# The inputs of a convolution transposed by VectorE and a DRAM round trip instead of TensorE, in a two-layer decoder trunk on one core

## The chip, the core and the metric

The kernel runs on one NeuronCore of a Trainium2 chip. Its engines each work through their own list of instructions in order: TensorE (PE; PEld is its weight load), VectorE (DVE), ScalarE (ACT), GpSimd (POOL) and SyncE (SP), which here issues nearly all DMAs. The metric is the device time of one execution in microseconds.

## The reference

A trunk of two layers over 256 tokens of width 1024, in float32. Each layer is a feed-forward block, a mixer and a second feed-forward block. The mixer projects the tokens once and splits the columns; one branch is a Mamba-2 scan, whose inputs go through a causal convolution of 4 taps over the tokens, one filter per channel (1536 channels):

```python
q, k, v, z, xbc, dt_raw, u, vg, gate_raw = jnp.split(xn @ w_in, split_at, axis=-1)
y_a = moba_attention(q, k, v)
xbc = jax.nn.silu(causal_depthwise_conv(xbc, conv_w, conv_b))
xs, bm, cm = jnp.split(xbc, [SSM_WIDTH, SSM_WIDTH + SSM_GROUPS * SSM_STATE], axis=-1)
y_s = ssd_scan(xs, dt, a, bm, cm) + d_skip[:, None] * xs
y_s = rms_norm(y_s.reshape(b_, s, SSM_WIDTH) * jax.nn.silu(z), ssm_norm_g)
```

## The kernel before

The 256 tokens are two tiles (`t` = 0, 1) of 128. Every product of activations and weights is made of three matmuls of 128x512 (`unit`, L213 to L215), because both operands are split into a high and a low part: `hi*hi + lo*hi + hi*lo`. The weights come in blocks of 128x1024 (512 KB). For each block SP loads `raw` (L160), ScalarE makes `whi` from it (L180) and VectorE `wlo` (L181). There are 6 `raw` buffers and 11 pairs of parts; the split of a new block waits for TensorE to be through with the block whose pair it takes, and the load of a new `raw` waits for the `wlo` that frees its buffer. A block is 12 matmuls on TensorE.

Everything else runs as tasks beside these matmuls. The order on every engine is the order in which the code is run through: after each unit (6 matmuls, counted as 1.3 us) `pump` lets the tasks go on whose waits have run out, then starts at most one split. The wait after a `yield` comes from the table `W` (`x0` 0.65, `cv` 5.2, `cs` 6.5, `out` 6.5, `in` 6.5, and so on). `finish` runs a task to its end at once, whatever its waits: what is left of it is then written in one piece into the engines' lists.

In the mixer, `project` makes 512 columns at a time into PSUM. First come two chunks of `xbc` together, then `conv(0)` and `conv(1)` are spawned; then the third chunk, and `conv(2)`; then two chunks of `z` (4 blocks each); then `finish(*cv)` (L910), and on to `q`. One `conv`:

1. `tokens` (L504, ScalarE) scales the two PSUM tiles into `xtok`, 128 tokens x 512 channels each.
2. `transposed` (L513 TensorE, L516 ScalarE) turns them by four 128x128 transposes a tile into the PSUM tile `ctr` and copies that into `xc`, channels x tokens.
3. ScalarE scales `xc` by the last tap (L535, four instructions), VectorE adds the three shifted taps (L541, six instructions, a wait, six more), ScalarE applies the SiLU (L544).
4. For chunks 0 and 1, eight transposes on TensorE (L552, `xstr`) and two copies on ScalarE (L553) bring the result back to tokens x channels; for chunk 2, two transposes (L559, `btr`) and a copy (L561).

The feed-forward blocks have a transpose of another kind: `swap_out` and `swap_in` (L277 to L286). VectorE transposes 32x32 blocks inside a 128x512 tile, SP writes the tile to DRAM and reads it back with the blocks in their places.

Of the kernel before, what the change touches and what calls it, by code (L numbers as in the profile page):

```python
# [9 lines left out]
F32 = mybir.dt.float32  # L10
# [6 lines left out]
P = 128  # L17
L = 2
S = 256
NT = S // P  # L20
# [27 lines left out]
W = {'gw': 6.5, 'tr': 0, 'parts': 0, 'sq': 1.3, 'lead': 3.9, 'sq2': 5.2, 'hh': 5.2, 'x0': 0.65, 'cv': 5.2, 'cs': 6.5, 'xs': 0, 'dt1': 2.6, 'dt2': 0, 'dt3': 5.2, 'cb': 2.6, 'w1': 1.3, 'w2': 5.2, 'ys': 3.9, 'qk': 3.9, 'vv': 0, 'qs': 0, 'ex': 0, 'p1': 10.4, 'p2': 0, 'p3': 3.9, 'ge': 0, 'ln': 10.4, 'sv': 0, 'yc': 9.1, 'mg': 3.9, 'out': 6.5, 'in': 6.5}  # L48
# [3 lines left out]
def trunk(ctx, tc, a):  # L52
    nc = tc.nc
    V, A, G, T = nc.vector, nc.scalar, nc.gpsimd, nc.tensor
# [5 lines left out]
    dram = ctx.enter_context(tc.tile_pool(name="dram", bufs=1, space=bass.MemoryType.DRAM))  # L60
# [3 lines left out]
    def b4(name, shape=(P, 1024), dt=F32):  # L64
        return big.tile(list(shape), dt, name=name, tag="b4", bufs=B4)

    def b2(name, shape=(P, 512), dt=F32):
        return big.tile(list(shape), dt, name=name, tag="b2", bufs=B2)
# [15 lines left out]
    def tr(name):  # L84
        return psum.tile([P, 512], F32, name=name, tag="tr", bufs=TR)
# [196 lines left out]
    def swap_in(dst, rd):  # L282

        v = rd.rearrange("(a i) (c e) -> c i a e", a=4, c=4)
        for c in range(4):
            nc.sync.dma_start(dst[32 * c:32 * c + 32], v[c])  # L286

    def halves(ps, hi, lo):

        p3 = ps.rearrange("p (k t) -> p k t", k=4)  # L290
        A.copy(hi, p3)
        V.tensor_tensor(lo, p3, hi.bitcast(F32), op=ALU.subtract)
# [185 lines left out]
    def mixer(l, x, r2, nxt):  # L478
# [20 lines left out]
        def tokens(ps, scales, name):  # L499

            out = []
            for t in range(NT):
                o = b2(name)
                A.activation(o, ps[t], AF.Copy, scale=scales[t])  # L504
                out.append(o)
            return out

        def transposed(toks, place, eng):

            for t in range(NT):  # L510
                ps = tr("ctr")
                for j in range(4):
                    T.transpose(ps[:, j * P:(j + 1) * P], toks[t][:, j * P:(j + 1) * P], ident)  # L513
                p3 = ps.rearrange("p (k t) -> p k t", k=4)
                if eng == "a":
                    A.copy(place(t), p3)  # L516
                else:
                    V.tensor_copy(place(t), p3)
                yield W["tr"]
# [6 lines left out]
        def conv(c, ps):  # L526
            toks = tokens(ps, r2, "xtok")
            xc = b4("xc", (P, 4, S))
            yield W["x0"]
            yield from transposed(toks, lambda t: xc[:, :, t * P:(t + 1) * P], "a")  # L530
            o = b4("conv", (P, 4, S))
            w = lambda j, k: pl[:, G_CW + 4 * (4 * c + j) + k:G_CW + 4 * (4 * c + j) + k + 1]
            for j in range(4):
                ct = 4 * c + j
                A.activation(o[:, j, :], xc[:, j, :], AF.Identity, scale=w(j, 3),  # L535
                             bias=pl[:, G_CB + ct:G_CB + ct + 1])
            for jj in (0, 2):
                for k in range(3):
                    s = 3 - k
                    for j in (jj, jj + 1):  # L540
                        V.scalar_tensor_tensor(o[:, j, s:], xc[:, j, :S - s], w(j, k), o[:, j, s:],  # L541
                                               op0=ALU.mult, op1=ALU.add)
                yield W["cv"]
            A.activation(o, o, AF.Silu)  # L544
            yield W["cs"]
            if c < 2:
                for t in range(NT):
                    if t not in xs:
                        xs[t] = b4(f"xs{t}")
                    pt = tr("xstr")  # L550
                    for j in range(4):
                        T.transpose(pt[:, j * P:(j + 1) * P], o[:, j, t * P:(t + 1) * P], ident)  # L552
                    A.copy(xs[t][:, 512 * c:512 * c + 512], pt)  # L553
                    yield W["xs"]
            else:
                bc["T"] = o
                pt = tr("btr")
                for g in range(SG):
                    T.transpose(pt[:, g * P:(g + 1) * P], o[:, g, 0:P], ident)  # L559
                bc["b"] = b2("btok", (P, SG * P))  # L560
                A.copy(bc["b"], pt[:, :SG * P])  # L561
# [184 lines left out]
        def attention(yax, free):  # L746
            for t in range(NT):
# [33 lines left out]
                for g in range(2):  # L781
                    yield W["p1"]
                    pts = {}
                    for k in range(t + 1):
                        pt = tr("ptr")
                        for j in range(4):
                            T.transpose(pt[:, j * P:(j + 1) * P], sc[g][:, j, k * P:(k + 1) * P], ident)
                        pts[k] = b2("pT", (P, 4, P))
                        A.copy(pts[k], pt.rearrange("p (h q) -> p h q", h=4))
                        yield W["p2"]  # L790
                    yield W["p3"]
                    po = tr("pv")
                    for j in range(4):
                        hh = 4 * g + j
                        for k in range(t + 1):
                            T.matmul(po[:, j * P:(j + 1) * P], vv[k][:, hh * HD:(hh + 1) * HD], pts[k][:, j, :],
                                     start=k == 0, stop=k == t)
                    halves(po, hi[:, 4 * g:4 * g + 4, :], lo[:, 4 * g:4 * g + 4, :])
# [106 lines left out]
        for c, ps in enumerate(project("xbc", head=HOLD, nch=2)):  # L905
            cv.append(spawn(conv(c, ps)))
        factors()
        cv.append(spawn(conv(2, project("xbc")[0])))
        ze = [spawn(z_evac(c, project("z")[0])) for c in range(2)]
        finish(*cv)  # L910
# [224 lines left out]
```

## Time and profile before

| | |
|---|---|
| median of three runs | 1486.49 us (1485.8 to 1487.09) |
| the profiled execution | 1487.98 us, of which the span of instructions is 1486.2 us |
| TensorE busy | 1472.1 us, 99% of the span |
| VectorE, ScalarE busy | 955.2 us (64%), 782.6 us (53%) |
| DMA | 293.37 MB, a mean of 197 GB/s |

The page gives for each engine the time in which it was busy, and the chain of work that ended last, followed back from the end: which engine each piece of it was spent on. Times inside the profile count from the first instruction. The convolutions of the first layer lie between 215 and 253 us, those of the second between 950 and 988 us.

### The profile page before, as it was taken

The page shows a single profiled execution, that of the slowest core. Times are in us where ns is not written, and L with a number is a line of the kernel's source. Part 1 is how long each engine was busy: PE and PEld are TensorE (multiplying, and loading weights), DVE is VectorE, ACT ScalarE, POOL GpSimd, SP SyncE. Part 2 cuts the span into 40 slices and gives each one's busy share as a digit, 9 for nine tenths or more (in the row PEclk, how much of TensorE's full clock was granted, in tenths as well). Part 3 has the DMA queues.
Part 4 walks back from the last instruction along what each step waited for, and adds up shares of the span by engine and source line. Part 5 has one row for each costly group of instructions (what it writes and reads, how often), then busy time and mean ns, then how long its engine had stood idle before and what let it go on. Part 6 is the DMA issues. An engine that isn't in the chain of part 4 may idle for free.

```text
span 1486.2 us, 18786 instructions
## 1 busy us (share of the span) xinstructions
PE 1472.1 (99%) x6850; PEld 1218.8 (82%) x6850; DVE 955.2 (64%) x1160; ACT 782.6 (53%) x1079; POOL 55.6 (4%) x98
## 2 busy tenths in 40 slices
PE   9999999999999999999999999999999999999998
PEld 7888888878888888888888888888788888888886
DVE  6766477766666857656486564876665667676652
ACT  6644367555374536544364543765554645464441
POOL 0000020000000000000000000200000000000000
PEclk9999999999999999999999999999999999999999
DMA  8987655335556445888568784654354564478860
GB/s 291 323 253 236 199 190 179 127 115 184 159 181 217 168 154 198 283 230 259 163 230 256 235 253 132 224 167 135 119 192 141 194 204 170 134 272 261 238 200 29
DMA packets 112476, 293.37 MB, mean 197 GB/s; under 512 B 16896, under 2 KB 41600, under 8 KB 112384
## 3 DMA queue, kind: packets, MB, share of 16 engines
q1 hardware_dynamic: 111808, 291.84, 60.6%
q8 instruction: 54, 0.88, 0.2%
q10 hardware_dynamic: 576, 0.33, 0.1%
q14 instruction: 38, 0.31, 0.1%
HBM read 279.54 MB, written 12.58 MB: 197 GB/s over the span
## 4 chain that ended last, share of the span: by engine, by line
PE 94%; DVE 4%; ACT 1%; issue 1%; POOL 0%; DMA 0%; DVEq 0%; ACTq 0%; POOLq 0%
PE gu L213 11%; PE gu L215 11%; PE gu L214 11%; PE dn L213 5%; PE dn L215 5%; PE dn L214 5%; PE br L213 3%; PE br L215 3%; PE br L214 3%; PE gate L215 2%; PE gate L213 2%; PE gate L214 2%; DVE wlo L181 2%; PE xbc L215 1%; PE xbc L213 1%; PE xbc L214 1%
## 5 line engine op out<-in xcount | busy, mean ns | idle before, releaser
L181 DVE TENSOR_TENSOR wlo<-raw,whi 128x1024 fp32r<-128x1024 f32 x495 | 600.2, 1232 | 331.1 <-ACT whi L180 319.8
L180 ACT CAST whi<-raw 128x1024 fp32r<-128x1024 f32 x495 | 512.8, 1051 | 380.9 <-PE gu L215 131.8
L213 PE MATMUL gu<-whi,xh 128*128 128x512 f32 x704 | 276.0, 392 | 1.4 <-ACT xh L316 1.4
L214 PE MATMUL gu<-wlo,xh 128*128 128x512 f32 x704 | 274.9, 391 | 0.0
L215 PE MATMUL gu<-whi,xl 128*128 128x512 f32 x704 | 274.8, 390 | 0.0
L213 PEld LDWEIGHTS gu<-whi,xh 128*128 128x128 f32 x704 | 132.7, 188 | 29.8 <-ACT xh L316 1.8
L215 PEld LDWEIGHTS gu<-whi,xl 128*128 128x128 f32 x704 | 132.6, 188 | 28.0 <-DVE xl L317 0.4
L214 PEld LDWEIGHTS gu<-wlo,xh 128*128 128x128 f32 x704 | 132.5, 188 | 27.9 <-DVE wlo L169 0.9
L213 PE MATMUL dn<-whi,hTh 128*128 128x512 f32 x352 | 137.5, 391 | 0.0
L215 PE MATMUL dn<-whi,hTl 128*128 128x512 f32 x352 | 137.0, 389 | 0.0
L214 PE MATMUL dn<-wlo,hTh 128*128 128x512 f32 x352 | 136.9, 389 | 0.0
L215 PEld LDWEIGHTS dn<-whi,hTl 128*128 128x128 f32 x352 | 66.1, 188 | 13.8
L213 PE MATMUL gate<-whi,xh 128*128 128x512 f32 x192 | 77.3, 403 | 0.0
L214 PEld LDWEIGHTS dn<-wlo,hTh 128*128 128x128 f32 x352 | 66.1, 188 | 13.5
L213 PEld LDWEIGHTS dn<-whi,hTh 128*128 128x128 f32 x352 | 66.1, 188 | 13.4
L215 PE MATMUL gate<-whi,xl 128*128 128x512 f32 x192 | 75.0, 391 | 0.0
L214 PE MATMUL gate<-wlo,xh 128*128 128x512 f32 x192 | 74.8, 390 | 0.0
L316 ACT CAST xh<-xg 128x512 fp32r<-128x512 f32 (+1 forms) x25 | 15.1, 603 | 62.3 <-DVE xg L314 62.3
L215 PEld LDWEIGHTS gate<-whi,xl 128*128 128x128 f32 x192 | 36.0, 188 | 7.7
L405 ACT ACTIVATE silu<-gu,r 128x512 f32<-128x512 f32 (+1 forms) x48 | 31.3, 654 | 19.8 <-PE gu L215 16.2
L214 PEld LDWEIGHTS gate<-wlo,xh 128*128 128x128 f32 x192 | 36.2, 188 | 6.6
L213 PEld LDWEIGHTS gate<-whi,xh 128*128 128x128 f32 x192 | 36.1, 188 | 6.6
(243 smaller groups left out, 2248.3 us busy)
## 6 DMA issues: line engine op xcount, KB each, us to landing
raw<-in_mix SPq DMA_DIRECT2D x232, 512.0 KB, 4.2
raw<-in_gu SPq DMA_DIRECT2D x175, 512.0 KB, 4.9
raw<-in_dn SPq DMA_DIRECT2D x88, 512.0 KB, 4.5
swap<-xt SPq DMA_DIRECT2D x40, 256.0 KB, 3.2
hr<-swap SPq DMA_DIRECT2D x160, 64.0 KB, 4.9
row_ffn_post_g<-in_ffn_post_g SPq DMA_DIRECT2D x4, 512.0 KB, 7.0
swap<-xt SPq DMA_DIRECT2D x8, 128.0 KB, 4.4
hr<-swap SPq DMA_DIRECT2D x32, 32.0 KB, 6.1
```

The costliest lines, as they stand in the source:

```text
L180: A.copy(hi, w)
L181: V.tensor_tensor(lo, w, hi.bitcast(F32), op=ALU.subtract)
L213: T.matmul(o, xh(k, t), hi[:, off:off + n], start=first, stop=False)
L214: T.matmul(o, xh(k, t), lo[:, off:off + n], start=False, stop=False)
L215: T.matmul(o, xl(k, t), hi[:, off:off + n], start=False, stop=last)
L316: A.copy(o_h, xg)
L405: A.activation(silu[t][:, :w], gate(t), AF.Silu, scale=r2[t])
```

## The change

Step 2 of `conv` is replaced, in both layers and for all three chunks. VectorE transposes each `xtok` tile in blocks of 32x32 (`V.transpose`), SP writes it into a DRAM tile in the order channels x tokens by four DMAs, one for each 32 partitions, and after a wait one DMA reads the whole chunk back as `xc`. The waits before and after are other ones too.

```diff
+    def swap_whole(toks, o):
+
+        rd = dram.tile([4, P, S], F32, name="swapw", tag="swapw", bufs=6)
+        v = rd.rearrange("k (c i) (t a j) -> t a i (k c) j", c=4, a=4, t=NT)
+        for t in range(NT):
+            xt = b2("xt")
+            V.transpose(xt, toks[t])
+            for b in range(4):
+                nc.sync.dma_start(v[t, b], xt[32 * b:32 * b + 32, :].rearrange("p (b j) -> p b j", j=32))
+        yield W["out"]
+        nc.sync.dma_start(o, rd.rearrange("k p e -> p k e"))
...
         def conv(c, ps):
             toks = tokens(ps, r2, "xtok")
             xc = b4("xc", (P, 4, S))
-            yield W["x0"]
-            yield from transposed(toks, lambda t: xc[:, :, t * P:(t + 1) * P], "a")
+            yield 2.6
+            yield from swap_whole(toks, xc)
+            yield W["in"]
             o = b4("conv", (P, 4, S))
```

The order of the instructions moves with it. The lines of the changed kernel are 12 or 13 higher: its L516 is L504 of before, L548 is L535, L557 is L544, L565 is L552, L566 is L553, L572 is L559, L574 is L561 and L658 is L645.

TensorE at the end of `z`, first layer, before (L552 and L559 are the transposes behind the convolution; the two pieces of `xstr` stand inside `z`):

```order
L552 MATMUL xstr<-con,conv 128x128 x8
...
L552 MATMUL xstr<-con,conv 128x128 x8
...
L214 MATMUL z<-wlo,xh_1706 128x512
L215 MATMUL z<-whi,xl_1707 128x512
L559 MATMUL btr<-con,conv 128x128 x2
L213 MATMUL q<-whi,xh_1619 128x512
```

and TensorE at the same place now:

```order
L214 MATMUL z<-wlo,xh_1706 128x512
L215 MATMUL z<-whi,xl_1707 128x512
L565 MATMUL xstr<-con,conv 128x128 x16
L572 MATMUL btr<-con,conv 128x128 x2
L213 MATMUL q<-whi,xh_1619 128x512
```

All sixteen `xstr` now stand behind the last `z`; the `ctr` of `xtok`, which stood further up (8, 8, 4 and 4), are gone.

ScalarE in the same stretch before, from the second chunk's copies to `btok` (`conv<-xc` is the scaling, `conv<-conv` the SiLU, `zs` takes `z` out of PSUM):

```order
L535 ACTIVATE conv<-xc,par 128x256 x8
L180 CAST whi<-raw 128x1024 x3
...
L535 ACTIVATE conv<-xc,par 128x256 x4
L180 CAST whi<-raw 128x1024
L544 ACTIVATE conv<-conv 128x1024 x2
...
L553 COPY xs_2213<-xstr 128x512 x2
L544 ACTIVATE conv<-conv 128x1024
L180 CAST whi<-raw 128x1024 x2
L561 COPY btok<-btr 128x256
```

and now:

```order
L548 ACTIVATE conv<-xc,par 128x256 x8
...
L548 ACTIVATE conv<-xc,par 128x256 x4
L180 CAST whi<-raw 128x1024
L557 ACTIVATE conv<-conv 128x1024
L566 COPY xs_2229<-xstr 128x512
L566 COPY xs_2236<-xstr 128x512
L557 ACTIVATE conv<-conv 128x1024
L566 COPY xs_2229<-xstr 128x512
L566 COPY xs_2236<-xstr 128x512
L557 ACTIVATE conv<-conv 128x1024
L574 COPY btok<-btr 128x256
```

The scalings stand later among the `whi` than before, and the three SiLUs, which stood apart, now alternate with the copies of `xstr` behind the last `whi` of the stretch.

SP now, where before there was an unbroken row of `raw` loads (the brackets say which counters an instruction waits for; DMAHW0 to DMAHW7 are those of earlier DMAs, DVE that of VectorE):

```order
L160 DMA raw<-in_mix 128x1024 [waits DMAHW7_49,DVE_49]
L296 DMA swapw<-xt 32x16x32 [waits DVE_49]
L296 DMA swapw<-xt 32x16x32
L296 DMA swapw<-xt 32x16x32 [waits DMAHW0_49]
...
L296 DMA swapw<-xt 32x16x32 [waits DMAHW5_49]
L160 DMA raw<-in_mix 128x1024 [waits DMAHW6_49,DVE_49]
L160 DMA raw<-in_mix 128x1024 [waits DMAHW7_49,DVE_49]
L160 DMA raw<-in_mix 128x1024 [waits DMAHW0_49,DVE_49]
L298 DMA xc<-swapw 128x4x256 [waits DMAHW1_49,PE_49]
L298 DMA xc<-swapw 128x4x256 [waits DMAHW4_49,DMAHW3_49,DMAHW5_49,DMAHW2_49,PE_49]
L160 DMA raw<-in_mix 128x1024 [waits DVE_49]
L296 DMA swapw<-xt 32x16x32 [waits DVE_49]
```

Sixteen writes stand in one piece, then three loads of weights, the reads of chunks 0 and 1, one load, the eight writes of chunk 2, three loads and its read.

## Rows read from the trace of the kernel before

**Rows 1.** The page: busy time of each engine; the chain that ended last, by engine.
```profile
PE 1472.1 (99%) x6850; PEld 1218.8 (82%) x6850; DVE 955.2 (64%) x1160; ACT 782.6 (53%) x1079; POOL 55.6 (4%) x98
...
PE 94%; DVE 4%; ACT 1%; issue 1%; POOL 0%; DMA 0%; DVEq 0%; ACTq 0%; POOLq 0%
```
**Rows 2.** Timeline of TensorE, first layer: start us, length us, instruction, count.
```profile
218.36 1.03 PE L513 MATMUL ctr<-con,xtok 128*128 128x128 f32 x8
219.15 0.48 PE L213 MATMUL xbc<-whi,xh 128*128 128x512 f32 x1
...
240.15 0.39 PE L213 MATMUL z<-whi,xh 128*128 128x512 f32 x1
...
245.36 0.39 PE L215 MATMUL z<-whi,xl 128*128 128x512 f32 x1
245.59 1.03 PE L552 MATMUL xstr<-con,conv 128*128 128x128 f32 x8
...
252.85 0.38 PE L559 MATMUL btr<-con,conv 128*128 128x128 f32 x2
252.99 0.48 PE L213 MATMUL q<-whi,xh 128*128 128x512 f32 x1
```
**Rows 3.** Timeline of TensorE, second layer.
```profile
952.89 1.04 PE L513 MATMUL ctr<-con,xtok 128*128 128x128 f32 x8
...
987.52 0.48 PE L213 MATMUL q<-whi,xh 128*128 128x512 f32 x1
```
**Rows 4.** Groups by line: shape, count | busy us, mean ns | idle before.
```profile
L277 DVE STREAM_TRANSPOSE xt<-hh 128x512 f32<-128x512 f32 (+1 forms) x48 | 29.0, 642 | 0.0
...
L544 ACT ACTIVATE conv<-conv 128x1024 f32<-128x1024 f32 x6 | 6.2, 1057 | 0.0
```
**Rows 5.** Timeline of ScalarE, first layer; in brackets idle time and its releaser.
```profile
222.22 4.08 ACT L535 ACTIVATE conv<-xc,par 128x256 f32<-128x256 f32 x8
...
228.50 1.06 ACT L180 CAST whi<-raw 128x1024 fp32r<-128x1024 f32 x1 [0.32 <-PE xbc L215]
...
246.23 1.07 ACT L553 COPY xs<-xstr 128x512 f32<-128x512 f32 x2 [2.10 <-PE xstr L552]
...
253.05 1.05 ACT L180 CAST whi<-raw 128x1024 fp32r<-128x1024 f32 x1 [1.60 <-PE z L215]
```
**Rows 6.** Timeline of VectorE, first layer.
```profile
221.44 1.23 DVE L181 TENSOR_TENSOR wlo<-raw,whi 128x1024 fp32r<-128x1024 f32 x1 [0.70 <-ACT whi L180]
222.91 4.91 DVE L541 SCALAR_TENSOR_TENSOR conv<-xc,par,conv 128x253 f32<-128x253 f32 x12 [0.25 <-ACT conv L535]
```
**Rows 7.** DMA issues by line: count, KB each, median us from issue to landing.
```profile
hr<-swap SPq DMA_DIRECT2D x32, 32.0 KB, 6.1
...
out<-h SPq DMA_DIRECT2D x2, 128.0 KB, 1.8
```
**Rows 8.** Timeline of SP: the first loads, and the reads of one `swap_in`.
```profile
1.16 0.42 SPq L958 DMA_DIRECT2D raw<-in_gu  x1
1.63 0.42 SPq L960 DMA_DIRECT2D h<-in_x  x1
...
46.53 6.41 SPq L286 DMA_DIRECT2D hr<-swap  x8
```
**Rows 9.** Windows: length, busy us of PE, PEld, DVE, ACT, POOL, clock, DMA share, GB/s.
```profile
38.00:39.00 1.00, 1.00 (x6) 0.81 (x5) 0.74 (x2) 0.62 (x2) 0.00 (x0) 1.00 1.01 410
...
475.50:476.75 1.25, 1.25 (x7) 1.03 (x6) 1.08 (x1) 0.14 (x1) 0.00 (x0) 1.00 1.12 339
```
**Rows 10.** Timeline of TensorE after a later wait, and one window there (clock last but two).
```profile
308.72 0.49 PE L680 MATMUL seg<-acsr,sel 128*128 128x512 f32 x1 [0.81 <-DVE xg L314]
310.79 0.63 PE L513 MATMUL ctr<-con,qtok 128*128 128x128 f32 x4 [1.58 <-DVE ssw L682]
...
312.33 0.63 PE L214 MATMUL k<-wlo,xh 128*128 128x512 f32 x1
...
311.50:315.50 4.00, 4.00 (x12) 3.14 (x11) 3.45 (x4) 1.94 (x4) 0.00 (x0) 0.57 0.00 0
```

## The prediction, written before the changed kernel ran

> **What bounds the kernel now.** I read the page's busy times and its chain of waits first: the reader is to see that TensorE is busy for 99% of the span and carries 94% of the chain [rows 1]. An instruction taken off TensorE is therefore worth its own length, and a wait put in front of TensorE costs its full length. Then the timeline of TensorE through the stretch that is changed, from the third chunk of `xbc` to the first matmul of `q`. The 24 matmuls of `z` from 240.15 to 245.36 start 5.21/23 = 0.2265 us apart [rows 2]. The `ctr` transposes follow twelve matmuls of the third chunk, so that chunk starts at 218.36 - 12 x 0.2265 = 215.64 us; I call this E. From E to the first `q` at 252.99 are 37.35 us [rows 2]. The twelve weight blocks in between (4 of `xbc`, 8 of `z`) have 12 matmuls each: 144 x 0.2265 = 32.62 us. The rest, 4.73 us, is 42 transposes (24 `ctr`, 16 `xstr`, 2 `btr`), or 0.113 us each; the eight of the first row fit that (0.79 us to the next matmul, which then takes 0.09 us more than its neighbours) [rows 2]. The second layer repeats it: 952.89 - 2.72 = 950.17, and `q` at 987.52, again 37.35 us [rows 3]. So TensorE doesn't wait at all in this stretch today; the convolutions run beside it on the other engines.
>
> **What goes.** 48 transposes leave TensorE: 24 x 0.113 = 2.7 us a layer, 5.4 us in all, all of it on the bound engine. ScalarE loses the 12 copies of these transposes: they lie beside TensorE and are worth nothing by themselves. The PSUM tiles that become free are worth nothing either, since nothing waits for one here.
>
> **What comes.** VectorE gets 12 transposes; one of the FFN takes 642 ns [rows 4], so 3.7 us a layer. VectorE has room (64% busy), but it works in order, and the point is what stands behind. SP gets 24 write DMAs and 3 reads a layer. The three 128x512 token pairs of a layer each go out as 8 DMAs of 64 KB, each in 512 pieces of 128 bytes.
>
> **What moves, and where it lands.** By the waits in the code the chunks 0 and 1 now do their convolution 15 work units after they are handed over, not 4, and each unit is 6 matmuls (1.36 us). The order of the instructions shows what is left over at the end of `z`: on TensorE all 16 `xstr` and the 2 `btr` stand in one piece behind the last `z` and ahead of `q`; on ScalarE three SiLUs and four PSUM copies alternate there behind the last `whi`. TensorE ends `z` at E + 32.62 = 248.3, 2.0 us after which it would be at `q` with the 18 transposes that stay. It has to wait instead for this chain, each piece with its own row: the last `whi`, which cannot start before the last block of `z` is done (today it starts at 253.05, released by `z`) [rows 5]; a SiLU of 1.06 us [rows 4]; 0.2 us to the transposes, and 1.7 us from the start of the transposes to the end of the two copies (246.23 + 1.07 less the transposes' start at 245.59) [rows 2, 5]; SiLU and copies again for chunk 1; the SiLU of chunk 2; `btr`. That is 1.06 + 1.9 + 1.06 + 1.9 + 1.06 + 0.35 = 7.3 us from the first SiLU to `q`.
>
> When can the first SiLU start? **With transfers that are in time**, ScalarE goes: the `whi` that waits for the end of `xbc` at 228.50 today [rows 5] comes 1.8 us sooner, 226.7, since 16 `ctr` are gone; each further `whi` waits one block, 2.72 us; three of them end at 235.9; eight scalings, 4.08 us [rows 5], end at 240.0; `whi`, two `zs`, three `whi`, the last bound by TensorE, end at 246.8; four scalings 248.9; `whi` 249.9; SiLU 251.0. Chunk 2's SiLU also has to wait for VectorE: 12 shifted sums from 236.5 on, two `wlo` that wait for their `whi`, to 244.6, 12 sums (4.91 us [rows 6]) to 249.5, two `wlo` of 1.2 us 251.9, six sums 254.3, a `wlo` 255.5, six sums 258.0, SiLU 259.1, `btr`, and `q` at 259.4. That is 6.4 us later than today, with the 2.7 us saved already in it.
>
> **Are the transfers in time?** The transposes stand behind the `wlo` of 221.44 [rows 6], end 222.5 to 224.4, and the writes follow. Nothing in the trace writes 128-byte pieces to DRAM, so I bound the price of one DMA of 512 pieces. From below: its 64 KB at the 339 GB/s of the stretch in which the spatial weights arrive in 512-byte pieces [rows 9] are 0.19 us, but SP issues no faster than one in 0.47 us (1.16 to 1.63) [rows 8], so 0.47 us a DMA. In the middle: 339 GB/s in pieces of 512 bytes are 660 pieces a microsecond [rows 9]; if a piece of 128 bytes costs no less than one of 512, a DMA costs 512/660, 0.77 us. The landing times say the same: eight transfers may be under way at once (SP's waits, shown with the change, go round eight counters), and with the 6.1 us of the smallest `hr` reads [rows 7] each is 6.1/8 = 0.76 us. Eight `hr` reads behind weights take SP 6.41 us, 0.80 each [rows 8]. From above: 1.5 us, twice that, if a piece has to be read before it is written. I take 0.75 us, since three rows meet there.
>
> A transfer of 128 KB into an empty queue lands after 1.8 us [rows 7], 0.3 of them data, so 1.5 us are fixed; I count 1.3 of these behind the data. Then the 16 writes of chunks 0 and 1 occupy the queue from 223.2 to 235.2 and have landed at 236.5. Three weight blocks (512 KB at 410 GB/s [rows 9], 1.3 us each) were issued behind them, and the two reads of 512 KB (1.6 us each) behind those: `xc` of chunk 0 lands at 242.1 and that of chunk 1 at 243.8, where 235.9 was needed. Chunk 2's eight writes wait in SP behind the reads, go out from 243.8 to 249.8, land at 251.1; three weight blocks and the read follow, and its `xc` lands at 256.7, where 246.8 was needed. From there: four scalings 2.05, `whi` 1.03 and the chain of 7.3 us give `q` at 267.1; VectorE is done in time for that. That is **14.1 us** more a layer. The weights don't run out meanwhile: the splits are some nine blocks ahead (9 x 2.72 = 24 us), and SP fetches six more.
>
> **The clock.** After 0.81 and 1.58 us of idle around 310 today's matmuls go to 0.63 us, and the granted clock is 0.57 from 311.5 to 315.5, next to the lower level [rows 10]: 4 x 0.43 = 1.7 us lost. A stall of 14 us will do this too: 1.7 us a layer.
>
> **The sum** against the profiled execution (span 1486.2, own time 1487.98): 2 x (14.1 + 1.7) = 31.6 us, so a span of 1517.8. The median of the runs, 1486.49, is 1.5 us under that execution's time; so 1518.1 for the median.
>
> **Rivals.**
> - *The transfers are in time* (0.47 us a DMA or less): 2 x (6.4 + 1.7) = 16.2 us, 1503. Speaks for it: pieces are small in bytes. Against: 512 of them. If the pause also lets ScalarE and VectorE catch up so far that today's later stall of 2.4 us and its slow clock (4.1 us a layer) vanish, 8.2 us go off again: 1494.5.
> - *A piece costs double* (1.5 us a DMA): the same sums end chunk 2's `xc` at 274.7 and bring `q` to 285.1, 32.1 us late: 2 x (32.1 + 1.7) = 67.6 us, 1554. Nothing in the trace speaks against a dearer write; nothing shows one. By the Trainium skill ("DMA: Bandwidth & Descriptors", Specifications) a transfer under 512 bytes makes the DMA engine read, modify and write, which would be this case, 1554; no row here shows it.
> - *Faster*: the convolutions remain hidden and TensorE keeps its 5.4 us: 1481. This decides if the third SiLU is over at 250.1, when TensorE would be through with `xstr`. The place is the end of `z`; against it stands the order itself, in which the first SiLU is behind a `whi` that needs the last `z`.
> - *The change doesn't take TensorE's transposes away*: excluded by the order of the instructions, in which no `ctr` of `xtok` is left.
>
> **How the numbers follow.** Forecast (0.6 to 1.1 us a DMA, 1507 to 1532) 0.52; in time (1494 to 1507) 0.15; double and dearer 0.27, of which 0.07 over 1556; same 0.03; faster 0.03. The range 1498 to 1556 leaves out some 2 in 10. A measurement of this kernel tells 0.2% (3 us) from no change: slower 0.94, within 0.03, faster 0.03.
>
> **What would show it.** In the changed kernel's timeline TensorE should be idle between the last `z` and the first `xstr`, and again ahead of `btr`, released by ScalarE's SiLU, 15 to 20 us in all from the end of `z` to `q`, in both layers, with a granted clock near 0.5 after it. ScalarE's scaling should wait for the DMA of `xc`. Writes of `xt` should land some 5 to 7 us after issue when 16 are queued. I am wrong if the wait for `xc` is under 2 us (then the price of a piece is too high), if TensorE is late already inside `z` (then the weights were starved, by SP), or if other stalls later in the mixer shrink.

## The result, and the profile after

| | before | changed |
|---|---|---|
| median of four runs each | 1486.79 us | 1521.01 us (1520.57 to 1521.66) |
| ratio | 1 | 1.0229, 95% interval 1.0211 to 1.0247 |
| profiled execution, span | 1486.2 us | 1518.4 us |
| TensorE busy | 1472.1 us, 99% | 1474.4 us, 97% |

The kernel is slower by 34 us; the spans of the two profiled executions differ by 32.2 us. The page of the changed kernel, its busy times and the chain by engine, which answer to [rows 1]:

```profile
PE 1474.4 (97%) x6802; PEld 1219.4 (80%) x6802; DVE 960.7 (63%) x1172; ACT 778.7 (51%) x1067; POOL 55.7 (4%) x98
...
PE 90%; DVE 5%; ACT 2%; DMA 1%; issue 1%; POOL 0%; SPq 0%; DVEq 0%; ACTq 0%; POOLq 0%
```

TensorE has 48 instructions fewer and is busy 2.3 us longer: what was saved is outweighed by work that now runs at a lower clock. The chain has lost four points of TensorE and now goes over the other engines. Where, the waits say (engine, line, releaser: total us, times, longest):

```profile
PE xstr L565 <- ACT conv L557: 26.4, 4, 12.1
PE btr L572 <- ACT conv L557: 3.3, 2, 1.6
```

These two are new, 29.7 us, and all in the place of [rows 2, 3]. Behind them the view lists the waits of before, ahead of `seg` and a later `ctr`, the same to 0.1 us (1.6 and 3.1 us). The timeline of TensorE there, first layer (start, length, instruction, in brackets idle time and its releaser):

```profile
259.77 1.97 PE L565 MATMUL xstr<-con,conv 128*128 128x128 f32 x8 [11.08 <-ACT conv L557]
263.37 1.97 PE L565 MATMUL xstr<-con,conv 128*128 128x128 f32 x8 [1.63 <-ACT conv L557]
266.98 0.69 PE L572 MATMUL btr<-con,conv 128*128 128x128 f32 x2 [1.63 <-ACT conv L557]
```

Eight `xstr` take 1.97 us where they took 1.03 [rows 2]. The releaser is the SiLU on ScalarE, whose timeline shows what it waited for itself:

```profile
242.56 4.06 ACT L548 ACTIVATE conv<-xc,par 128x256 f32<-128x256 f32 x8 [6.38 <-DMA xc<-swapw]
...
255.74 2.08 ACT L548 ACTIVATE conv<-xc,par 128x256 f32<-128x256 f32 x4 [4.19 <-DMA xc<-swapw]
257.73 1.03 ACT L180 CAST whi<-raw 128x1024 fp32r<-128x1024 f32 x1
258.67 1.05 ACT L557 ACTIVATE conv<-conv 128x1024 f32<-128x1024 f32 x1
```

And SP, which issues the transfers that these wait for (start, length of the group, instructions):

```profile
222.78 11.21 SPq L296 DMA_DIRECT2D swapw<-xt  x16
234.08 1.41 SPq L160 DMA_DIRECT2D raw<-in_mix  x3
235.58 1.15 SPq L298 DMA_DIRECT2D xc<-swapw  x2
236.78 0.99 SPq L160 DMA_DIRECT2D raw<-in_mix  x1
237.81 8.93 SPq L296 DMA_DIRECT2D swapw<-xt  x8
246.84 2.77 SPq L160 DMA_DIRECT2D raw<-in_mix  x3
249.83 0.38 SPq L298 DMA_DIRECT2D xc<-swapw  x1
```

What holds the last read is not the eight writes ahead of it. They end at 246.74, but the third of the loads behind them starts at 249.28 only: it waits for the `wlo` on VectorE that frees its buffer, and that `wlo` (248.04 to 249.26) stands behind the twelve sums of chunks 0 and 1. The read stands behind that load in SP's list. In the second layer the chain of work shows the same (start, length, what):

```profile
995.08 2.12 DVE conv L554 x6
997.93 1.14 DVE wlo L181
999.09 0.33 SPq L160
999.63 6.13 DMA xc<-swapw
```

So the line runs backwards from TensorE: `xstr`, SiLU, scaling, read of chunk 2's `xc`, the load of weights ahead of it, `wlo` and the sums of chunks 0 and 1 on VectorE, their scaling, their two reads, three loads of weights, sixteen writes. Chunk 2's eight writes lie beside it, with 1.2 to 1.4 us to spare. Last, windows over the wait and behind it (length, busy us of PE, PEld, DVE, ACT, POOL, granted clock, DMA share, GB/s):

```profile
252.00:268.00 16.00, 4.96 (x20) 4.07 (x21) 11.78 (x25) 8.54 (x14) 1.90 (x1) 0.50 0.55 183
268.00:272.00 4.00, 4.00 (x27) 3.35 (x26) 0.00 (x0) 1.24 (x3) 0.00 (x0) 0.53 0.01 4
272.00:276.00 4.00, 4.00 (x31) 3.23 (x28) 0.57 (x1) 2.00 (x3) 0.00 (x0) 1.00 0.00 0
```

The clock is at its lower level, 0.50, in the wait, and TensorE's first 4 us of unbroken work behind it run at 0.53 of full speed, which costs 4 x 0.47 = 1.9 us.

**The account.** As a measure for all kernels here I take the time from the first `xtok` on ScalarE (the convolution's inputs are there) to the first `q` and to the first `k` on TensorE; each is the difference of two starts in the timelines, first and second layer.

| kernel | to q, us | to k, us |
|---|---|---|
| before | 36.9, 36.9 | 66.4, 66.4 |
| changed | 50.9, 51.9 | 82.4, 83.8 |
| without the writes | 42.7, 43.6 | 74.3, 75.6 |
| transposes on TensorE, new order | 45.3, 45.2 | 76.0, 76.5 |
| each write twice | 63.8, 63.2 | 95.7, 94.2 |
| long pieces | 48.8, 48.8 | 79.8, 80.2 |
| matmuls in the wait | 51.7, 49.5 | 83.3, 80.4 |
| convolutions end behind half of q | (moved) | 80.7, 82.3 |
| the same, dt ahead of z | (moved) | 71.5, 73.1 |
| without the first wait | 50.3, 50.0 | 81.9, 80.9 |
| no transposes at all | 34.1, 34.1 | 63.6, 63.6 |
| one chunk | 36.1, 36.0 | 65.6, 65.5 |
| two chunks, new order | (moved) | 70.1, 68.9 |
| before, new order | (moved) | 69.4, 70.9 |

In the changed kernel `q` is 14.1 and 15.0 us later, `k` 16.0 and 17.4: the 2 us in between are the slow clock. 33.4 us together, of the span's 32.2; the other -1.2 lie outside the stretch. There the slow clock behind the later wait [rows 10] comes in some layers and not in others, 1.6 us each time: from the first `k` to the first `v` this kernel takes 32.9 us in the first layer and 34.4 in the second, before 34.5 in both.

### The profile page after: what moved, and what is told of

It reads as the page before. It is cut to its first block, busy times and chain, and to the rows that moved or that the text cites. A ratio compares the mean times of both kernels' runs of the same rounds, so it can differ in the third digit from the quotient of the medians.

```text
span 1518.4 us, 18775 instructions
## 1 busy us (share of the span) xinstructions
PE 1474.4 (97%) x6802; PEld 1219.4 (80%) x6802; DVE 960.7 (63%) x1172; ACT 778.7 (51%) x1067; POOL 55.7 (4%) x98
## 4 chain that ended last, share of the span: by engine, by line
PE 90%; DVE 5%; ACT 2%; DMA 1%; issue 1%; POOL 0%; SPq 0%; DVEq 0%; ACTq 0%; POOLq 0%
PE gu L213 10%; PE gu L214 10%; PE gu L215 10%; PE dn L215 5%; PE dn L213 5%; PE dn L214 5%; PE br L215 3%; PE br L213 3%; PE br L214 3%; DVE wlo L181 2%; PE gate L215 2%; PE gate L213 2%; PE gate L214 2%; PE xbc L213 1%; PE xbc L215 1%; PE xbc L214 1%
## 5 line engine op out<-in xcount | busy, mean ns | idle before, releaser
L213 PEld LDWEIGHTS gate<-whi,xh 128*128 128x128 f32 x192 | 36.1, 188 | 6.5
```

Source lines behind the costliest of these rows:

```text
L213: T.matmul(o, xh(k, t), hi[:, off:off + n], start=first, stop=False)
```

## The experiments

Each ran on the same chip as a new set of runs of the kernel before, and ratios are to that. From chip to chip the medians of the kernel before lie between 1486.39 and 1488.33 us, so a difference between two runs of different chips is good to 1 or 2 us.

### Without the writes

```diff
...
-            for b in range(4):
-                nc.sync.dma_start(v[t, b], xt[32 * b:32 * b + 32, :].rearrange("p (b j) -> p b j", j=32))
...
-        nc.sync.dma_start(o, rd.rearrange("k p e -> p k e"))
+        nc.sync.dma_start(o, a["mix"][0, 0].rearrange("p (k e) -> p k e", k=4))
```

> The changed kernel without its 48 writes; the six reads of 512 KB stay where they are but fetch a block of weights, so the convolution works on wrong inputs and its result is left out of the output's meaning. Theory (the writes are what makes the inputs late; the new order costs the rest): the inputs are in time, ScalarE and VectorE alone keep TensorE waiting at the end of z, q is 6 to 7 us later than in the kernel before and 2 us a layer go to the clock: 1502 to 1507 us. Rival 1 (the order alone costs nothing, only the transfers do): 1481 to 1487. Rival 2 (the writes don't matter, the order alone does it): 1518 to 1522.

1504.1 us, ratio 1.0109 (1.0093 to 1.0125). The theory holds: `q` is 5.9 and 6.7 us later than before, not 14 to 15. ScalarE waits for the last read 1.3 us, and TensorE still waits at each step of the same chain:

```profile
252.37 1.09 PE L561 MATMUL xstr<-con,conv 128*128 128x128 f32 x8 [3.72 <-ACT conv L553]
255.14 1.97 PE L561 MATMUL xstr<-con,conv 128*128 128x128 f32 x8 [1.68 <-ACT conv L553]
257.63 1.06 ACT L553 ACTIVATE conv<-conv 128x1024 f32<-128x1024 f32 x1
258.74 0.69 PE L568 MATMUL btr<-con,conv 128*128 128x128 f32 x2 [1.63 <-ACT conv L553]
```

The third row is the third SiLU, on ScalarE: it starts without a wait, and VectorE's last sums had ended 0.4 us before, at 257.25.

So the loss has two halves. About 16 us come without the writes, from the new order with the reads and VectorE's transposes still in it, and with what TensorE saves already taken off. About 18 us come with the writes.

### The transposes on TensorE, in the new order

```diff
-            yield W["x0"]
+            yield 2.6
+            yield W["out"]
             yield from transposed(toks, lambda t: xc[:, :, t * P:(t + 1) * P], "a")
+            yield 4.0
```

> The kernel before with its transposes on TensorE, but at the places to which the change moves the work (no transposes by VectorE, no transfers through DRAM). Theory (the place of the convolution behind the last z costs by itself): TensorE waits some 6 to 9 us a layer at the end of z and loses about 2 us a layer to the clock: 1502 to 1510 us. Rival (only the round trip through DRAM costs): 1486 to 1488, with no wait ahead of xstr.

1506.59 us, ratio 1.0127 (1.0110 to 1.0145). The theory holds again, from the other side: without any exchange through DRAM, and with the 48 transposes still on TensorE, the later place of the convolution costs some 18 us. The waits of TensorE are the same two lines:

```profile
PE xstr L554 <- ACT conv L546: 7.9, 4, 2.3
PE btr L561 <- ACT conv L546: 4.8, 2, 2.8
```

### Each write twice

```diff
+        r2nd = dram.tile([4, P, S], F32, name="swapx", tag="swapx", bufs=6)
+        v2 = r2nd.rearrange("k (c i) (t a j) -> t a i (k c) j", c=4, a=4, t=NT)
...
-            for b in range(4):
-                nc.sync.dma_start(v[t, b], xt[32 * b:32 * b + 32, :].rearrange("p (b j) -> p b j", j=32))
+            for r in (v, v2):
+                for b in range(4):
+                    nc.sync.dma_start(r[t, b], xt[32 * b:32 * b + 32, :].rearrange("p (b j) -> p b j", j=32))
```

> The changed kernel with every write issued twice, the second time to a DRAM tile that nobody reads; 24 writes more a layer, of which 16 stand ahead of the reads of chunks 0 and 1 and 8 more ahead of chunk 2's. Theory (the writes are in one line with the reads, and each costs the 0.70 us that SP takes for one): 24 x 0.70 = 16.8 us a layer later at xc of chunk 2, TensorE waits as much longer: 1552 to 1556 us. Rival (writes lie beside something else that takes as long, such as the loads of weights): under 1535 us.

1545.04 us, ratio 1.0392 (1.0376 to 1.0408), 24 us above the changed kernel: between the theory and its rival. The writes are in the line, but one more costs less than the 0.70 us I read from SP. ScalarE's two waits for `xc`:

```profile
250.67 4.04 ACT L551 ACTIVATE conv<-xc,par 128x256 f32<-128x256 f32 x8 [14.57 <-DMA xc<-swapw]
...
268.53 2.07 ACT L551 ACTIVATE conv<-xc,par 128x256 f32<-128x256 f32 x4 [8.90 <-DMA xc<-swapw]
```

Against the changed kernel's 242.56 and 255.74 these are 8.1 us for 16 more writes and 12.8 us for 24: 0.51 and 0.53 us each. In the second layer they are 7.8 and 11.3 us, 0.49 and 0.47 each. The figure of chunks 0 and 1 is the cleaner one, since at chunk 2 VectorE has a share in the time. SP's groups say the same once the line is running:

```profile
222.64 2.89 SPq L299 DMA_DIRECT2D swapw<-xt  x4
225.57 3.25 SPq L299 DMA_DIRECT2D swapx<-xt  x4
228.92 2.10 SPq L299 DMA_DIRECT2D swapw<-xt  x4
231.06 2.14 SPq L299 DMA_DIRECT2D swapx<-xt  x4
```

The first eight take 0.77 us each, the later ones 0.53. The 0.70 was a mean over a slow start behind loads of weights and a faster rest.

### The same writes in long pieces

```diff
-        v = rd.rearrange("k (c i) (t a j) -> t a i (k c) j", c=4, a=4, t=NT)
+        v = rd.rearrange("k (h i r) e -> (k h) i (r e)", h=2, r=2)
...
-                nc.sync.dma_start(v[t, b], xt[32 * b:32 * b + 32, :].rearrange("p (b j) -> p b j", j=32))
+                nc.sync.dma_start(v[4 * t + b], xt[32 * b:32 * b + 32, :])
```

> The changed kernel with the same 48 writes of 64 KB, but each goes to one stretch of the DRAM tile in row order, in pieces of 2048 bytes and not of 128 (the convolution then works on inputs in a wrong order, and the output isn't that of the reference). Theory A (the prediction's: the price of the 512 pieces makes the inputs late): the wait for the last xc falls by 6 us a layer or more, 1505 to 1510 us. Theory B (from the trace of after, where SP needs 0.70 us for one write and the queue could take more pieces: the number of DMAs, their issue and the loads of weights around them make the inputs late, the pieces cost little): 2 to 4 us a layer less, 1513 to 1518 us. Rival C (pieces cost nothing at all): 1520 to 1522 us.

1513.87 us, ratio 1.0178 (1.0162 to 1.0193), 7 us under the changed kernel. Theory B holds: pieces sixteen times as long bring `q` forward by 2.1 and 3.2 us. The number of DMAs and what they queue with remain. SP in this run:

```profile
224.37 8.91 SPq L296 DMA_DIRECT2D swapw<-xt  x16
...
237.76 8.70 SPq L296 DMA_DIRECT2D swapw<-xt  x8
```

The sixteen need 0.56 us each, against 0.70 for the sixteen short ones at the same place in the changed kernel. Chunk 2's eight need 8.70 us, nearly the 8.93 of the changed kernel: their pieces don't set that time. What does is to be seen in SP's waits of this run:

```profile
SPq L296 <- DMA raw<-in_mix: 7.5, 8, 1.4
SPq L296 <- DMA xc<-swapw: 5.8, 4, 2.2
```

The eight stand behind two reads and four loads of 512 KB, and each waits until the DMA eight places ahead of it has landed. In the changed kernel no wait for a DMA shows there; the issue itself is long. (For 3.8 us in all its waits name VectorE, but the transposes that these writes send had ended at 233.4.) The eight writes of chunk 2 by their line (count: ns of one, minimum, median and maximum, first and last start):

```profile
L296 SPq DMA_DIRECT2D swapw<-xt x8: 488/826/2041, 237.8 to 246.2; - x8
```

With large transfers under way ahead of it, a write in 128-byte pieces takes SP up to 2.04 us. In a row of their like SP takes 0.50 us for one of these and 0.42 for one in long pieces (medians of nine and of eight writes), 0.55 and 0.47 from start to start. So short pieces cost issue time, but little, and at this place both kinds land only behind the transfers ahead of them.

What the pieces cost the 16 DMA engines themselves can be read in two stretches with such writes alone, first the changed kernel, then this run (the last two figures are the DMA engines' busy share and GB/s):

```profile
231.50:234.50 3.00, 3.00 (x15) 2.46 (x14) 2.84 (x4) 1.06 (x1) 0.53 (x1) 1.00 0.78 120
231.00:234.00 3.00, 3.00 (x15) 2.49 (x14) 1.53 (x2) 1.05 (x1) 0.53 (x1) 1.00 0.58 145
```

Short pieces keep the engines 78% busy for 120 GB/s, long ones 58% for 145, so a byte in short pieces takes 1.6 times as long. Where writes have piled up behind loads the factor is 2: the first eight of the changed kernel land 0.37 us apart (228.6 to 231.2), the first seven of this run 0.18 (229.4 to 230.5). Both are less than SP's 0.47 to 0.55 us from one write to the next, so in a free row SP sets the pace, and most of the price doesn't show.

### Matmuls in the wait

```diff
+        dummy = tr("dummy")
+        for _ in range(44):
+            T.matmul(dummy, x.h(0, 0), x.x.hi[0][:, 0:4, :], start=True, stop=True)
         finish(*cv)
```

> The changed kernel with 44 matmuls of 128x512 a layer whose result nobody uses, placed on TensorE between the last z and the first xstr, where it waits 11 to 12 us. Theory (part of the loss is the half clock of xstr, btr and the first matmuls of q behind the wait): the granted clock stays near 1 there, the chain of SiLUs and copies is shorter by 1 to 1.5 us and q starts at full speed, 3 to 3.5 us a layer less: 1513 to 1516 us. Rival (the wait alone sets the time, TensorE's clock is not on the path): 1520 to 1522.

1515.78 us, ratio 1.0183 (1.0159 to 1.0207). The time is in the theory's range, but the trace supports only a part of it:

```profile
248.47 10.13 PE L925 MATMUL dummy<-xh 128*128 128x512 f32 x44
260.79 1.09 PE L565 MATMUL xstr<-con,conv 128*128 128x128 f32 x8 [2.19 <-ACT conv L557]
263.57 1.97 PE L565 MATMUL xstr<-con,conv 128*128 128x128 f32 x8 [1.68 <-ACT conv L557]
```

The first eight `xstr` run at full speed, 0.9 us less, and then the clock is down again, so `q` starts at half speed as in the changed kernel: 0.75 in the window from 260 to 264, 0.50 from 264 to 272. I had expected it to stay up. To `k` the first layer takes 0.9 us longer than in the changed kernel: its last `xc` came 1.6 us later, counted from `xtok`, and the 0.9 us of the first `xstr` are gained. The second takes 3.4 us less: 1.6 us by an earlier `xc`, 0.9 by the first `xstr`, and 1.0 between `q` and `k`, where the slow clock ends sooner. So what can be put down to the clock is 0.9 us a layer, and 1.0 more in one of them. The profiled execution is 3.1 us faster than that of the changed kernel, and these terms give 2.6. That the median is 5 to 7 us faster isn't explained by it and stays open; the four executions lie between 1510.64 and 1517.67 us.

### The end of the convolutions behind the first half of q

```diff
-        finish(*cv)
         dte = spawn(dt_task(wdt[l]))
         at = [spawn(qk_evac("q", 0, project("q")[0]))]
+        finish(*cv)
```

> The changed kernel with the end of the convolutions moved behind the first projection of q (11 us of matmuls). Theory (the loss is TensorE waiting at this one place, and other work of TensorE covers it): the wait of 11 to 12 us ahead of xstr shrinks to under 4 us and the three later ones stay or go: 1483 to 1497 us, and under 1487 if nothing is left of the wait. Rival (the transfers slow the kernel wherever they stand, by late weights or late buffers): 1510 or more, with the wait at another place.

1518.82 us, ratio 1.0202 (1.0183 to 1.0221). The theory fell, and the rival's time came true, though not for its reason: the weights were not late. The wait moved:

```profile
PE dtps L592 <- ACT dtT L585: 14.7, 2, 8.4
```

On ScalarE, first layer:

```profile
256.52 2.08 ACT L548 ACTIVATE conv<-xc,par 128x256 f32<-128x256 f32 x4 [4.30 <-DMA xc<-swapw]
...
262.48 0.34 ACT L585 COPY dtT<-dtps 32x256 f32<-32x256 f32 x1
```

`dtT` is a copy of 0.3 us that has nothing to do with the convolution. But on ScalarE, which works in order, it stands behind chunk 2's scaling, and that waits for the DMA of `xc`; TensorE needs `dtT` in the middle of `q`. I had asked what covers TensorE's wait and not what else stands in ScalarE's line.

### The same, with dt ahead of z

```diff
+        dte = spawn(dt_task(wdt[l]))
         ze = [spawn(z_evac(c, project("z")[0])) for c in range(2)]
-        finish(*cv)
-        dte = spawn(dt_task(wdt[l]))
         at = [spawn(qk_evac("q", 0, project("q")[0]))]
-        finish(dte, *ze)
+        finish(*cv, dte, *ze)
```

> The changed kernel with the end of the convolutions behind the first projection of q, as in the run that did only this, and the task of dt moved ahead of z, so that no copy of dt stands behind the waiting scalings on ScalarE. Theory (that run didn't gain because ScalarE works in order and passed the wait on to the dt transposes): that wait of 6 to 8 us is gone, TensorE waits about 1.5 us for the first SiLU and some 4 us ahead of btr, 1490 to 1500 us. Rival (the wait turns up in full at another place again): 1512 us or more.

1500.45 us, ratio 1.0092 (1.0078 to 1.0106), just outside the range. With `dtT` out of the line the wait ahead of `dtps` is gone, and 20 of the 34 us with it. What is left is mainly chunk 2, whose SiLU now waits for VectorE's sums (2.9 us of ScalarE's time in the first layer), not for a transfer:

```profile
PE btr L572 <- ACT conv L557: 11.5, 2, 5.8
```

### Without the first wait

```diff
-            yield 2.6
             yield from swap_whole(toks, xc)
```

> The changed kernel without the wait of 2.6 ahead of VectorE's transposes, so that the writes start some 4 us earlier; scalings and SiLUs stand a little earlier on ScalarE with it, two SiLUs together ahead of xstr. Theory (TensorE's wait is the end of one line: writes, loads, reads, scalings, SiLUs): the 4 us come off the wait, and 1 to 2 us more for the two SiLUs in one piece, 1506 to 1513 us. Rival (SP or VectorE holds the writes back to their old time): 1518 to 1522 us.

1515.8 us, ratio 1.0192 (1.0176 to 1.0209): less than the theory asked. The writes do start 4.5 us earlier, but the gain isn't handed on:

```profile
218.31 11.44 SPq L296 DMA_DIRECT2D swapw<-xt  x16
...
231.81 1.70 SPq L298 DMA_DIRECT2D xc<-swapw  x2
...
245.84 1.15 DVE wlo L181
247.00 0.33 SPq L160
247.55 6.39 DMA xc<-swapw
...
265.17 1.06 ACT L556 ACTIVATE conv<-conv 128x1024 f32<-128x1024 f32 x1 [3.19 <-DVE conv L553]
```

(The first two rows are SP's timeline, the next three the chain of work, the last ScalarE's timeline.) Of 4.5 us at the first write, 3.8 are left at the first reads and 2.3 when the first of them lands; four loads stand ahead of them now, not three. The 2.3 are still there at the last read: again a load waits for a `wlo` on VectorE, and the read behind it, while chunk 2's eight writes, though slower (10.30 us), had ended by 245. ScalarE starts the last scaling 1.8 us earlier. Then the third SiLU waits 3.2 us for VectorE's sums, which in the changed kernel had ended 2 us before it was ScalarE's turn, and `q` is 0.6 us earlier in the first layer and 2.0 in the second. So the theory's line left out VectorE, which stands in it twice: by the `wlo` ahead of the last read, and by the last sums ahead of the third SiLU.

### What the transposes are worth

```diff
-                ps = tr("ctr")
-                for j in range(4):
-                    T.transpose(ps[:, j * P:(j + 1) * P], toks[t][:, j * P:(j + 1) * P], ident)
-                p3 = ps.rearrange("p (k t) -> p k t", k=4)
+                if eng != "n":
+                    ps = tr("ctr")
+                    for j in range(4):
+                        T.transpose(ps[:, j * P:(j + 1) * P], toks[t][:, j * P:(j + 1) * P], ident)
+                p3 = (toks[t] if eng == "n" else ps).rearrange("p (k t) -> p k t", k=4)
...
-            yield from transposed(toks, lambda t: xc[:, :, t * P:(t + 1) * P], "a")
+            yield from transposed(toks, lambda t: xc[:, :, t * P:(t + 1) * P], "n")
```

> The kernel before without the 48 transposes of xtok: ScalarE copies the untransposed xtok into xc at the same places, so the convolution works on untransposed inputs and the output isn't that of the reference. It is what the change would give if its whole path were hidden. Theory (an instruction taken off TensorE is worth its own length, 2.7 us a layer): 1480.5 to 1483 us. Rival (another engine, or the weights, sets the end of this stretch as soon as TensorE has less to do, and nothing is gained): 1485.5 to 1488 us.

1481.92 us, ratio 0.9967 (0.9954 to 0.9979). The theory holds: 5 us, of 5.4 worked out. In the trace `q` is 2.8 us earlier in both layers, and `k` as well, so nothing else became late.

### One chunk, and two

```diff
-            yield W["x0"]
-            yield from transposed(toks, lambda t: xc[:, :, t * P:(t + 1) * P], "a")
+            if c == 0:
+                yield from swap_whole(toks, xc)
+                yield W["in"]
+            else:
+                yield W["x0"]
+                yield from transposed(toks, lambda t: xc[:, :, t * P:(t + 1) * P], "a")
```

> The change for chunk 0 alone, with its write at once (no wait of 2.6 ahead of it); chunks 1 and 2 are transposed on TensorE as in the kernel before, at the old places. 8 writes and one read a layer. Theory (the exchange itself is right, only its transfers don't fit behind three chunks): the inputs of chunk 0 are in time, no wait ahead of xstr, and 8 transposes a layer are saved, 8 x 0.113 x 2 = 1.8 us: 1484 to 1486 us. Rival (any use of this path puts a wait on TensorE, by the order on ScalarE or VectorE): 1489 to 1500 us with an idle TensorE at the end of z.

1486.52 us, ratio 0.9993 (0.9984 to 1.0002). No wait of TensorE is new in this stretch, and `k` comes 0.8 and 0.9 us earlier: the eight transposes. That the whole kernel gains 1.8 us by it is neither shown nor excluded, the interval reaches from -2.4 to +0.3 us. Then two chunks, with the order of the run with dt ahead of `z`, and that order alone on the kernel before:

```diff
-            if c == 0:
+            if c < 2:
                 yield from swap_whole(toks, xc)
...
+        dte = spawn(dt_task(wdt[l]))
         ze = [spawn(z_evac(c, project("z")[0])) for c in range(2)]
-        finish(*cv)
-        dte = spawn(dt_task(wdt[l]))
         at = [spawn(qk_evac("q", 0, project("q")[0]))]
-        finish(dte, *ze)
+        finish(*cv, dte, *ze)
```

> The order of the run with dt first and the convolutions ending behind the first projection of q; chunks 0 and 1 go through DRAM, with their writes at once, and chunk 2 is transposed on TensorE at its old place. Theory (the exchange pays exactly where the whole round trip is covered by work of TensorE): no idle TensorE ahead of xstr or btr, 16 transposes a layer saved, 16 x 0.113 x 2 = 3.6 us: 1482 to 1485 us, faster than both kernels. Rival (with 16 writes the scalings on ScalarE still wait for xc and pass it on to dt, z or the weights behind them): 1488 to 1500 us with a wait of 2 us or more at one of these places.

> The kernel before with the same new order (dt ahead of z, the convolutions ending behind the first projection of q), all transposes on TensorE. It tells what the order is worth without the exchange. Theory (TensorE waits nowhere in this stretch in the kernel before, so the order has nothing to give): 1485.5 to 1488 us. Rival (the order itself brings the gain of the run beside it): 1482 to 1485 us.

1491.94 us, ratio 1.0033 (1.0020 to 1.0046), and 1492.88 us, ratio 1.0037 (1.0024 to 1.0049). Both theories fell. The order itself costs 5 us: `xstr` then waits 4.8 us in all for ScalarE's copies, and the 16 transposes of two chunks don't show beside that; 70.1 and 68.9 us to `k` against 69.4 and 70.9 leave the sign open. In the run with two chunks ScalarE's line is held by VectorE, which has the sums of the convolution ahead of what the dt task needs:

```profile
255.75 0.18 ACT L648 ACTIVATE eac<-acs 128x16 f32<-128x16 f32 x1 [7.97 <-DVE nacs L646]
...
257.71 1.27 ACT L661 ACTIVATE zs<-z,r 128x512 f32<-128x512 f32 x2
```

`zs`, which frees the PSUM that `q` needs, stands behind it, and TensorE waits 1.2 us a layer ahead of `q`; ahead of `xstr` it waits 4.1 us in all. In the run with the order alone the same wait of ScalarE is 3.1 us. I found no version that beats both kernels.

## Why the prediction was right

The forecast was 1518 us and the measurement 1521, and the mechanism that was forecast is in the main the one that came: TensorE is idle between the last `z` and the first `xstr` and again ahead of `btr`, ScalarE's scalings wait 6.38 and 4.19 us for the DMA of `xc`, and the clock is at 0.50. One piece of the line was not the one forecast, and the nearness of the two numbers is partly luck. By its steps:

- **What bounds.** Right: TensorE, with no slack in this stretch. The saved transposes are worth their length, 5 us in the run without them.
- **The order at the end of z.** Right, and the firmest part. The case in which the transfers are in time was worked out as 1503 and `q` at 259.4; the run without writes gave 1504.1 and a first `q` at 259.08. That these are so near is luck in part: the forecast had VectorE's sums end last, at 258.0, while in the run they were done at 257.25 and the last to come was ScalarE, held up 1.3 us by a read and by `xstr` at the low clock. The run with TensorE's transposes in the new order confirms that it is the order.
- **The chain from the first SiLU to q.** Under-sized: 7.3 us forecast, 267.32 - 258.67 = 8.65 us measured. I had the row at 1.03 us for eight `xstr` and reckoned the low clock only behind the wait, not in it, where each eight take 1.97 us.
- **The price of a write.** Over-sized, and so the step that failed: 0.75 us, where one more write costs 0.49 to 0.51 us. The three rows that met at 0.75 were of loads and reads [rows 7 to 9]; none was of writes, and the `hr` reads have 128 pieces each and not 512. The eight `hr` reads of 6.41 us also hold 2.7 us in which SP waits for loads to land, so that row gives no price at all. The lower bound was misread too: SP's 0.47 us is no limit, since the same trace has starts 0.36 us apart (at 1376.86). That the three agreed was taken for more than it was. Writes in the changed kernel land 2.8 us after issue at the median (DMA issues: KB each, median us to landing), not 5 to 7; of the sixteen only the first four, behind loads, take that long.

```profile
swapw<-xt SPq DMA_DIRECT2D x48, 64.0 KB, 2.8
```

- **The time at which xc is there.** Right to about 1 us, and partly by luck: chunks 0 and 1 forecast 242.1 and 243.8, scaling from 242.56; chunk 2 forecast 256.7, scaling from 255.74. At the sixteen writes the dear price stood in for a slow start (0.77 us each for the first eight, behind loads). At chunk 2 the forecast let the eight writes and the loads behind them set the time; what set it was VectorE, by the `wlo` for which the load ahead of the read waits, and for that the prediction had no term. Had I put the 0.53 us of a long row into the same sum, with nothing for these, 24 x 0.22 = 5.3 us a layer would have been missing from the forecast.
- **The double price.** The Trainium skill ("DMA: Bandwidth & Descriptors", Specifications) says that a transfer under 512 bytes makes the DMA engine read, modify and write. The runs here show a price, but nothing like the 1.5 us of that case: where writes have piled up, one in 128-byte pieces takes the DMA engines 0.37 us and one in 2048-byte pieces 0.18, and SP's own 0.47 to 0.55 us a write hide most of the difference. The long pieces saved 2 to 3 us a layer. Whether the factor of 2 comes from reading before writing or from the number of pieces is not shown.
- **The clock.** 1.7 us a layer forecast from [rows 10], 1.9 to 2.4 measured. Right in size; the one attempt to buy it back, with dummy matmuls, kept the clock up for eight transposes a layer and no further.
- **The weights.** Right: no wait of TensorE for weights is new.

The sum was right because two errors of about 1 us a layer, the transfers too late and the chain too short, nearly cancel: 14.1 us a layer forecast, 14.1 and 15.0 measured.

## What to carry to other kernels

Work that leaves the bound engine is worth its length only where everything that replaces it ends before that engine arrives; work out the whole line, transfers, the engines' orders and the last serial chain, before counting the gain. When such a wait is moved under cover, ask for each in-order engine that takes part what unrelated instruction stands behind the waiting one, since that instruction's customers will wait next. SyncE is such an engine too: here a read stood behind a load that waited for VectorE. And price a transfer from rows of its own direction and shape: three rows of another kind that agree are still of another kind.

## What was not expected of the hardware

- Writes of 512 pieces of 128 bytes to DRAM go at one in 0.53 us in a long row, so some 970 pieces a microsecond, where loads in pieces of 512 bytes had shown 660 [rows 9]. The 0.53 us are set by SP's issue, about 0.50 us for 512 pieces and 0.42 for 32; where writes had piled up, the DMA engines took 0.37 us for one of 512 pieces and 0.18 for one of 32.
- What SP takes to issue a DMA is set by its neighbours: eight writes of 64 KB took it 8.93 us behind reads and loads of 512 KB, and 8.70 us in long pieces (waits for landings included), against 4.3 us for eight in a row of their like.
- TensorE's clock fell after short waits too: in the run with matmuls in the wait, 10 us of them at the upper level (1.00 from 248 to 260) were followed by 2.19 us of idle time, eight transposes, still at full speed, and 1.68 us of idle time, and the next eight transposes ran at half (1.97 us), with 0.50 in the windows from 264 to 272.
